# A hybrid decoder layer on one core: norm work moved between two engines, and weight quarters split early and kept in DRAM

## The chip, the cores and the metric

The kernel runs on one core of a Trainium2 chip. The core has five engines that take their instructions in order, each from its own queue, and that meet through semaphores: TensorE (PE in the profile; PEld is its loading of weights), VectorE (DVE), ScalarE (ACT), GpSimd (POOL) and SyncE (SP), which here only issues transfers. ACT and POOL issue transfers too. The metric is the device time of one execution in microseconds, as the median of several runs.

## The reference

The reference computes one layer of a decoder in float32 on 1024 prompt rows and 8 sample rows, which share all weights; the model has 1024 columns. Cut to what matters:

```
x = layer_norm(a * x + 0.5 * swiglu(x, w1_1, w3_1, w2_1))
m = hybrid_mixer(x, states, w_in, ..., w_o)
x = layer_norm(a * x + m)
y = layer_norm(a * x + 0.5 * swiglu(x, w1_2, w3_2, w2_2))

swiglu(x)     = (silu(x @ w1) * (x @ w3)) @ w2          (1024 -> 2816 -> 1024)
layer_norm(x) = (x - mean) * rsqrt(var + eps) * g + b   (over the 1024 columns)
hybrid_mixer: proj = x @ w_in + b_in; an RG-LRU branch (convolution, gates, a linear
  recurrence) and a gated delta-rule branch with 8 heads (convolution, l2 norms, chunked
  recurrence, RMS norm); merged = sum of both, gated; result merged @ w_o
```

New recurrent and convolution states are outputs too, those of the 8 sample rows with a full state matrix per row and head among them.

## The kernel before, in words

**Layout.** All 1032 rows lie along the free dimension and the model's columns along the 128 partitions, as 8 blocks. The rows are cut into three chunks of 344 columns (four of 258 at the end). Activations are kept as a pair XH, XL, a value rounded for TensorE's fast float32 format and the rest; weights are split in the same way, in quarters of 128 × 512 values. A product is three matmuls: high by high, high by low, low by high.

**A weight quarter's way.** In `wload`, SP loads a raw quarter (tile `wraw`, three buffers, 256 KB), ACT copies it rounded into `wh`, and DVE or POOL subtracts to give `wl` (four buffers each). A buffer is written again when its last reader is done. Where `hold` is given, the halves go to tiles that are free at that time.

**Order.** A framework orders the instructions of each engine when the kernel is built, by the order of the program and by ready times that it estimates. Inside an engine's queue nothing overtakes. Generators mix two pieces of work by hand: each `yield` hands over.

**The stages.** (1) SwiGLU 1: two column blocks of its hidden layer (f = 0, 1) as plain products, then 19 blocks f = 2 to 20 with one level of Strassen's algorithm (`strassen`; 7 products of 4 × 2 × 3 matmuls at 258 columns), whose weight sums DVE makes and whose results POOL stores to DRAM. Then `ffnb1`: the hidden values come back in six groups and are multiplied by w2, and the result is gathered in ACC. (2) In the last group, `last_steps` goes chunk by chunk; each chunk has 8 units (one 128-column block m), and after a unit the class `LN` adds the unit to a running sum. The sums of a chunk are closed during the next chunk: `finish` is a generator whose first step takes the mean (a matmul with a tile of ones adds over the partitions, L176), subtracts it, squares and adds up; its second takes the variance total (L176 again); its third normalizes and makes XH and XL. Which unit of the next chunk each step stands behind is set in `last_steps` (units 0 and `LN_STEP` = 4; 5 in SwiGLU 2). The last chunk of norm 1 is closed in `kqv_first`, between the first projections of the mixer. (3) The mixer: 8 heads of the delta rule, mixed with a stream of projections, then the product by w_o with norm 2, again through `last_steps`; each unit there loads two quarters of w_o. `sample`, the single-step recurrence of the 8 sample rows, is a chain of small matmuls pinned in TensorE's order between the units' steps: `wait(n)` lets n slots pass, of which each contraction step of a unit (three matmuls) gives one in the first chunk and two later. (4) SwiGLU 2, like SwiGLU 1 but with f = 0, 1, 2 plain; f = 0 and 1 are computed on two chunks while the third chunk of norm 2 is closed. Norm 3 closes the last group in four chunks; the last of them uses the variant `tail`, with a shorter way to the end.

**Engines in the norms.** The running sum (seven adds for a chunk) is POOL's but for the last add; the squares' adds alternate between DVE and POOL; of the eight splits into XH and XL, those listed in `ON_POOL` have their subtraction on POOL. In the w_o stage the merge's splits (`msplit`) and the weights' subtractions alternate too. POOL also issues the stores of SwiGLU's hidden values, of norm 2's result X2 (eight per chunk, `L232`), and the loads of X2's quarters. The split is `act(h, x, AF.Copy)` at L88 and `tt(l, x, h.bitcast(F32), OP.subtract, eng)` at L91; these helpers give their lines to most steps of the profile.

## Time and profile before

| | |
|---|---|
| median of 3 runs | 2609.95 us (2608.35 to 2614.61) |
| the profiled execution | 2612.26 us |
| its span in the profile | 2610.5 us |
| mean granted TensorE clock | 0.986 |
| busy: TensorE, DVE, ACT, POOL | 2532.2, 1742.9, 1134.0, 467.4 us |
| moved by DMA | 208.65 MB, 80 GB/s in the mean |

The stages in the profiled execution: Strassen blocks of SwiGLU 1 from about 60 to 440 us, the w2 groups to 665, norm 1 with the last w2 group and the first projections from 665 to 746, heads and projections to about 1740, w_o with norm 2 to about 1895, the blocks of SwiGLU 2 to about 2310, w2 and the tail to the end. A busy engine is one with an instruction in it; a matmul at a lower granted clock counts as busy for longer. A step of one tile (128 × 344, for example) is followed by its engine, its source line and the tiles that it reads and writes.

### The profile page before, as it was taken

Reading aid. Unit: us, or ns where it says so; the run is one execution under the profiler, and the core shown is the slowest. Engines: PE = TensorE matmul, PEld = TensorE weight load, DVE = VectorE, ACT = ScalarE, POOL = GpSimd, SP = SyncE. Lnnn points to the kernel's source line nnn. Section 1 sums busy time; section 2 is a strip of 40 time slices with the busy share of each in tenths; the row PEclk is TensorE's granted clock in tenths of the full one; section 3 lists DMA queues with packets and bytes.
Section 4 is the critical chain, followed back from the end, with each engine's and each line's share of the span. In section 5 each row is a group of like instructions: output and inputs, shape, how many; then the busy total and the mean of one; then the engine's idle time right before and its main releaser. Section 6 shows DMA issues by size and latency. Waiting matters only on the chain.

```text
span 2610.5 us, 47260 instructions
## 1 busy us (share of the span) xinstructions
PE 2532.2 (97%) x18374; PEld 2485.7 (95%) x18374; DVE 1742.9 (67%) x3641; ACT 1134.0 (43%) x2426; POOL 467.4 (18%) x633
## 2 busy tenths in 40 slices
PE   9999999999999999999999999998799999999996
PEld 8999999999888999999999999988799999999996
DVE  7666665644696676777767686777766666656446
ACT  5323333221463736565564637635533333332125
POOL 2000000300432112111112121134521111121013
PEclk9999999999998999999999999999899999999998
DMA  6222222432101111111111111124453444333221
GB/s 228 82 76 83 79 79 75 116 98 86 46 30 47 36 49 45 38 50 36 54 37 53 34 57 37 47 89 132 124 154 102 120 123 111 102 117 111 82 69 66
DMA packets 151135, 208.65 MB, mean 80 GB/s; under 512 B 35632, under 2 KB 76080, under 8 KB 150912
## 3 DMA queue, kind: packets, MB, share of 16 engines
q1 hardware_dynamic: 126176, 156.24, 19.6%
q0 software_dynamic: 13904, 43.34, 6.0%
q10 hardware_dynamic: 10832, 6.07, 0.8%
q8 instruction: 144, 2.36, 0.4%
q14 instruction: 79, 0.65, 0.1%
HBM read 164.60 MB, written 40.99 MB: 79 GB/s over the span
## 4 chain that ended last, share of the span: by engine, by line
PE 83%; ACT 6%; DVE 6%; DMA 1%; issue 1%; POOL 1%; ACTq 0%; SPq 0%; DVEq 0%; POOLq 0%
PE ps_mm L132 34%; PE ps_g L132 13%; PE ps_g L298 10%; PE ps_mm L298 10%; PE ps_sq L298 8%; PE ps_g L892 2%; ACT L88 2%; DVE ACC L94 2%; PE ps_sq L778 2%; ACT lnq L88 1%; PE ps_g L778 1%; PE ps_g L784 1%; DVE ACC L91 1%; POOL s L91 1%; DVE wl L91 1%
## 5 line engine op out<-in xcount | busy, mean ns | idle before, releaser
L132 PE MATMUL ps_mm<-XH,wh 128*128 128x344 f32 x1656 | 558.3, 337 | 6.1 <-ACT wh L88 5.8
L132 PE MATMUL ps_mm<-XH,wl 128*128 128x344 f32 x1656 | 532.9, 322 | 0.0
L132 PE MATMUL ps_mm<-XL,wh 128*128 128x344 f32 x1656 | 532.6, 322 | 0.1
L88 ACT ACTIVATE wh<-wraw 128x512 fp32r<-128x512 f32 (+2 forms) x360 | 213.9, 598 | 408.8 <-PE ps_mm L132 140.9
L132 PEld LDWEIGHTS ps_mm<-XH,wh 128*128 128x128 f32 x1656 | 314.4, 190 | 9.6 <-ACT wh L88 5.8
L132 PEld LDWEIGHTS ps_mm<-XL,wh 128*128 128x128 f32 x1656 | 314.4, 190 | 1.8 <-DVE XL L91 0.6
L132 PEld LDWEIGHTS ps_mm<-XH,wl 128*128 128x128 f32 x1656 | 313.8, 190 | 0.4 <-DVE wl L91 0.2
L91 DVE TENSOR_TENSOR wl<-wraw,wh 128x512 fp32r<-128x512 f32 (+3 forms) x339 | 232.3, 688 | 42.5 <-ACT wh L88 38.4
L298 PE MATMUL ps_g<-CH,wh 128*128 128x258 f32 x740 | 209.0, 282 | 0.0
L298 PE MATMUL ps_g<-CH,wl 128*128 128x258 f32 x740 | 208.9, 282 | 0.0
L298 PE MATMUL ps_g<-CL,wh 128*128 128x258 f32 x740 | 208.7, 282 | 0.0
L88 ACT ACTIVATE wh<-S 128x512 fp32r<-128x512 f32 x148 | 93.4, 631 | 197.9 <-PE ps_sq L298 126.8
L298 PE MATMUL ps_mm<-XH,wh 128*128 128x258 f32 x592 | 167.2, 282 | 0.0
L298 PE MATMUL ps_mm<-XH,wl 128*128 128x258 f32 x592 | 166.9, 282 | 0.0
L298 PE MATMUL ps_mm<-XL,wh 128*128 128x258 f32 x592 | 166.8, 282 | 0.0
L353 POOL DMA_DIRECT2D gs<-G x74 | 40.5, 547 | 652.1 <-DVE G L91 604.2
L91 DVE TENSOR_TENSOR wl<-S,wh 128x512 fp32r<-128x512 f32 x148 | 102.3, 691 | 70.9 <-ACT wh L88 70.6
L88 ACT ACT_TABLE_LOAD x109 | 139.8, 1283 | 5.4 <-issue 2.6
L132 PE MATMUL ps_g<-gl,wh 128*128 128x344 f32 x444 | 142.2, 320 | 0.0
L132 PE MATMUL ps_mm<-gl,wh 128*128 128x344 f32 x444 | 142.0, 320 | 0.0
L132 PE MATMUL ps_g<-gh,wh 128*128 128x344 f32 x444 | 142.0, 320 | 0.0
L132 PE MATMUL ps_mm<-gh,wh 128*128 128x344 f32 x444 | 142.0, 320 | 0.0
(536 smaller groups left out, 6884.9 us busy)
## 6 DMA issues: line engine op xcount, KB each, us to landing
wraw<-w SPq DMA_DIRECT2D x164, 256.0 KB, 2.8
wraw<-w_in SPq DMA_DIRECT2D x128, 256.0 KB, 2.6
gr<-gs SPq DMA_DIRECT2D x84, 258.0 KB, 2.8
wr<-w SPq DMA_DIRECT2D x76, 256.0 KB, 2.6
gs<-G POOLq DMA_DIRECT2D x74, 258.0 KB, 2.6
wraw<-w_o SPq DMA_DIRECT2D x40, 256.0 KB, 2.8
x<-ACC POOLq DMA_DIRECT2D x24, 172.0 KB, 2.2
y<-ACC SPq DMA_DIRECT2D x32, 129.0 KB, 1.9
```

The lines of the kernel that those rows point to most:

```text
L88: return S.activation(out, in_, f, **kw)
L91: return (eng or V).tensor_tensor(out, a, b, op=op)
L94: return V.scalar_tensor_tensor(out, a, s, b, op0=op0, op1=op1)
L132: PE.matmul(p, a, b, start=(n == 0), stop=(n == 3 * nk - 1))
L298: PE.matmul(ps_[c], a[:, k, :], b, start=(start and n == 0), stop=(n == 11), skip_group_check=not start)
L353: G.dma_start(gs[f][:, s], x)
L778: x = PE.matmul(ck(p, i), a, b, start=True, stop=True)
L784: x = PE.transpose(ck(p, i), a, IDT)
L892: pin(PE.matmul(o[r, c, :], a(c), b(c), start=True, stop=True))
```

## The change

- `LN.add` and `finish`: every running sum and every add of squares is DVE's. `ON_POOL` is gone: all subtractions that make XL are DVE's. In norm 1 all eight blocks take the shorter form that four of them had (ACT makes XH with the bias, one fused DVE step makes XL). The deviation `rs` takes a buffer of the ring `s1` (three) instead of `mu`'s only one, except in the tail.
- `last_steps`: the mean step stands behind unit 1 (before: 0), the variance and normalizing steps behind unit 6 in all norms (before: 4, and 5 in SwiGLU 2). In SwiGLU 2's plain blocks the steps of the open norm stand in the first chunk of f = 0 and of f = 1. The first projections are reordered so that three products, not two, precede the variance total.
- `presplit`: after each of the 19 Strassen blocks of SwiGLU 1, two weight quarters are loaded by SP, split by ACT and DVE in the usual rings, and both halves are stored by POOL to DRAM (256 KB each). The 38 quarters are: 8 of w2_1's last group, 6 of w_in (the first head's k, q and v), 16 of w_o, 8 of w1_2 and w3_2 for f = 0 and 1.
- `fetch`: where these quarters are used, POOL loads both halves straight into `wh` and `wl` or into the held tiles: 124 transfers of 256 KB, 80 of them in w_o, where quarters are loaded again in each chunk. The raw loads, rounding copies and subtractions at these places are gone.
- The subtractions of w2_2's last group and of the merge are all DVE's. The five waits of the sample chain grow (12 to 16, 6 to 14, 6 to 14, 8 to 16, 6 to 14 slots).

```diff
-LN_STEP = 4
+LN_STEP = 6
-ON_POOL = (1, 3, 5, 7)
...
+    def whl(n=4):
+        return [wp.tile([128, n, 128], F32R, name=x, tag=x, bufs=4) for x in ("wh", "wl")]
+
+    def presplit(quads):
+        for key, src in quads:
+            raw = wp.tile([128, 4, 128], F32, name="wraw", tag="wraw", bufs=3)
+            nc.sync.dma_start(raw, src)
+            h, l = whl()
+            split(h, l, raw)
+            halves[key] = dr.tile([2, 128, 4, 128], F32R, name="hv", tag="hv" + key)
+            for i, x in enumerate((h, l)):
+                G.dma_start(halves[key][i], x)
+            yield
+
+    def fetch(key, nq=2, hold=None):
+        hl = []
+        for q in range(nq):
+            h, l = hold(4) if hold else whl()
+            for i, x in enumerate((h, l)):
+                G.dma_start(x, halves[key + "_%d" % q][i])
+            hl += [(h[:, k, :], l[:, k, :]) for k in range(4)]
+        return hl
...
+        ws = [quads("w2%d" % m, A["w2_1"][m][:, g[0]:g[0] + 4], 1) for m in range(KD)]
+        ws += [quads("in%d" % b, A["w_in"][b]) for b in (KC, QC, VC)]
+        ws += [quads("o%d" % m, A["w_o"][m]) for m in range(KD)]
+        ws += [quads("w%d%d" % (i, f), A["w%d_2" % i][f]) for f in range(2) for i in (1, 3)]
...
-                tt(self.s1, self.ys[0], y, OP.add, G)
-            elif 2 < n < (KD - 1 if self.tail else KD):
-                tt(self.s1, self.s1, y, OP.add, G)
-            elif n == KD and not self.tail:
-                tt(self.s1, self.s1, y, OP.add, V)
+                tt(self.s1, self.ys[0], y, OP.add)
+            elif 2 < n < (KD - 1 if self.tail else KD + 1):
+                tt(self.s1, self.s1, y, OP.add)
...
-                    tt(q[k % 2], q[k % 2], q[k], OP.add, (V, G)[k % 2])
+                    tt(q[k % 2], q[k % 2], q[k], OP.add)
...
-            rs = third("mu", w)
+            rs = third("mu" if self.tail else "s1", w)
...
-                if i in ON_POOL or self.gi == 2:
+                if self.gi == 2:
                     act(y, y, AF.Identity, bias=b_)
-                    split(h, l, y, G if i in ON_POOL else V)
-                    if self.gi == 2:
-                        G.dma_start(X2[:, k, self.s], y)
+                    split(h, l, y)
+                    G.dma_start(X2[:, k, self.s], y)
                     continue
...
+            if n == 2 and f < 2:
+                return [fetch("w%d%d" % (i, f), hold=hold) for i in (1, 3)]
...
-                if fin and f == 0 and t < 2:
-                    for _ in range(1 + t):
+                if fin and t == 0 and f < 2:
+                    for _ in range(1 + f):
                         next(fin)
...
                     strassen(f, w1, w3, up, cx, store)
...
+                    for _ in range(2 if pre else 0):
+                        next(pre, None)
...
-                            held[m] = w2load(m, eng=(V, G)[m % 2], hold=hold if n == 2 or m < 6 else None)
+                            if n == 1:
+                                held[m] = fetch("w2%d" % m, 1, hold if m < 6 else None)
+                            else:
+                                held[m] = w2load(m, hold=hold)
...
-                if fin and i == 0:
+                if fin and i == 1:
                     next(fin)
-                if fin and i == LN_STEP + (out is not None):
+                if fin and i == LN_STEP:
...
-                wk, wq = (wload(A["w_in"][b0], KD) for b0 in (KC, QC))
-                wv = wload(A["w_in"][VC], KD, hold=hold)
+                wk, wq = (fetch("in%d" % b0) for b0 in (KC, QC))
+                wv = fetch("in%d" % VC, hold=hold)
...
                 kq(0, 1)
+                kq(0, 2)
                 kq(1, 0)
                 next(fin)
                 next(fin)
                 kq(1, 1)
-                kq(0, 2)
...
-                    split(h[:, :n], l[:, :n], ACC[:, k, t * TC:t * TC + n], (V, G)[k % 2])
+                    split(h[:, :n], l[:, :n], ACC[:, k, t * TC:t * TC + n])
...
-                    recent[m] = wload(A["w_o"][m], KD, eng=(V, G)[m % 2])
+                    recent[m] = fetch("o%d" % m)
...
-        yield from wait(12)
+        yield from wait(16)
...
-        yield from wait(6)
+        yield from wait(14)
```

More of the change, by code (lines that the diff above doesn't have):

```diff
@@ L124, in wload, with quads, early_list @@
         return hl
+    halves = {}
+    def whl(n=4):
[18 more added lines that the diff above has]
+        return hl
+    def quads(key, src, n=2):
+        return [(key + "_%d" % q, src[:, 4 * q:4 * q + 4]) for q in range(n)]
+    def early_list():
+        g = GROUPS[-1]
+        ws = [quads("w2%d" % m, A["w2_1"][m][:, g[0]:g[0] + 4], 1) for m in range(KD)]
+        ws += [quads("in%d" % b, A["w_in"][b]) for b in (KC, QC, VC)]
+        ws += [quads("o%d" % m, A["w_o"][m]) for m in range(KD)]
+        ws += [quads("w%d%d" % (i, f), A["w%d_2" % i][f]) for f in range(2) for i in (1, 3)]
+        return [q for w in ws for q in w]
     def mm3_steps(p, w, xs, nk):
@@ L386, in ffn @@
             make = combos(up, *((A["x"], 2) if n == 1 else (X2, 0)))
+            pre = presplit(early_list()) if n == 1 else None
             spare = ["S"] * 3 + ["wr"] * 3 + ["s0", "rb"]
@@ L1246, in sample @@
         V.tensor_copy(KE[:, 0], K_)
-        yield from wait(6)
+        yield from wait(14)
         pq = psum("sq")
@@ L1274, in sample @@
         tt(M, OS, OS, OP.mult)
-        yield from wait(8)
+        yield from wait(16)
         pn = psum("sq")
@@ L1286, in sample @@
         nc.scalar.dma_start(RTD, rt)
-        yield from wait(6)
+        yield from wait(14)
         pn = psum("sq")
```

## The prediction, made before the changed kernel was run

> **What bounds the kernel now.** I read the page's first part, then a table of stretches, then the list of what the engines waited for, and last the groups and the timeline inside the stretches that are not full. From the page:
>
> ```profile
> span 2610.5 us, 47260 instructions
> PE 2532.2 (97%) x18374; PEld 2485.7 (95%) x18374; DVE 1742.9 (67%) x3641; ACT 1134.0 (43%) x2426; POOL 467.4 (18%) x633
> ```
>
> TensorE sets the time. It idles 2610.5 − 2532.2 = 78 us, and no edit here takes a matmul away, so the gain lies inside those 78 us and in the clock granted around them. The stretches that the change touches (columns: us, then busy PE, PEld, DVE, ACT, POOL with counts, granted clock, DMA share, GB/s):
>
> ```profile
> 60.00:440.00 380.00, 380.00 (x3165) 380.00 (x3164) 238.62 (x444) 121.26 (x231) 20.20 (x38) 1.00 0.24 77
> 665.00:746.00 81.00, 69.63 (x401) 65.68 (x401) 66.73 (x112) 46.55 (x85) 43.27 (x43) 0.97 0.16 47
> 1740.00:1895.00 155.00, 128.18 (x752) 121.63 (x751) 109.94 (x185) 80.07 (x173) 81.97 (x88) 0.90 0.39 121
> 2565.00:2610.50 45.50, 25.96 (x155) 23.14 (x153) 27.50 (x65) 26.64 (x56) 14.29 (x20) 0.82 0.21 70
> ```
>
> The first row is the Strassen blocks of SwiGLU 1: TensorE full at full clock, so they have nothing to give and can only lose. Norm 1 (665 to 746) idles 81 − 69.63 = 11.4 us and loses about 0.03 × 69.63 = 2.1 us to the clock: 13.5 us at stake. Norm 2 with the w_o stage (1740 to 1895) idles 26.8 us and loses 0.10 × 128.18 = 12.8 us: 39.6 us. The tail idles 19.5 us, much of it the closing chain of the last chunk. What TensorE waited for, over the span (line, releaser, us in total, times, longest), then L176 alone in norm 1 and in the tail:
>
> ```profile
> PE ps_sq L176 <- DVE s L91: 28.7, 12, 7.6
> PE ps_g L132 <- DVE wl L91: 4.8, 3, 4.1
> PE ps_sq L1238 <- DVE St L1233: 4.3, 1, 4.3
> PE ps_sq L1277 <- DVE kt L91: 1.9, 1, 1.9
> PE ps_mm L132 <- DVE m_lt L91: 1.6, 1, 1.6
> ...
> PE ps_sq L176 <- DVE s L91: 7.6, 4, 2.5
> ...
> PE ps_sq L176 <- DVE s L91: 10.2, 5, 4.8
> ```
>
> Two thirds of this is L176, the partition totals of the norms, which wait for sums; the rest is the sample group's small matmuls and weight splits. The largest single wait, 7.6 us, is the last variance total of norm 2. From the timeline (start, us, engine, step, and in brackets the idle time before it), what stood ahead of it:
>
> ```profile
> 1872.04 0.69 DVE L91 TENSOR_TENSOR w1S<-wraw,w1wr 128x512 fp32r<-128x512 f32 x1 [5.44 <-ACT w1wr L88]
> ...
> 1875.05 5.45 POOL L91 TENSOR_TENSOR s<-s,lnq 128x344 f32<-128x344 f32 x3 [10.59 <-ACT lnq L88]
> ```
>
> DVE stood 5.44 us behind the split of one of SwiGLU 2's first weights, whose raw load was late, and then POOL needed 5.45 us for three adds. Both causes are things that the change removes.
>
> **The change, part by part.** First, additions and splits move from POOL to DVE. Groups in norm 1 (the first six rows), in norm 2 (four) and over the span (the last):
>
> ```profile
> L91 POOL TENSOR_TENSOR s<-s,ACC 128x344 f32<-128x344 f32 x15 | 14.8, 986 | 2.6 <-DVE ACC L94 1.8
> L91 POOL TENSOR_TENSOR s<-s,lnq 128x344 f32<-128x344 f32 x9 | 10.7, 1184 | 17.1 <-ACT lnq L88 16.9
> L94 DVE SCALAR_TENSOR_TENSOR ACC<-ACC,LNT,mu 128x344 f32<-128x344 f32 x16 | 12.1, 793 | 0.6 <-ACT mu L88 0.6
> L91 DVE TENSOR_TENSOR ACC<-ACC,mu 128x344 f32<-128x344 f32 x24 | 14.0, 629 | 0.8 <-ACT mu L88 0.8
> L91 DVE TENSOR_TENSOR wl<-wraw,wh 128x512 fp32r<-128x512 f32 x5 | 4.6, 929 | 3.6 <-ACT wh L88 3.6
> L91 DVE TENSOR_TENSOR w2h<-wraw,w2h 128x512 fp32r<-128x512 f32 x3 | 3.4, 1174 | 0.8 <-ACT w2h L88 0.8
> ...
> L94 DVE SCALAR_TENSOR_TENSOR ACC<-ACC,LNT,mu 128x344 f32<-128x344 f32 x24 | 20.1, 886 | 3.8 <-ACT mu L88 3.8
> L91 DVE TENSOR_TENSOR wl<-wraw,wh 128x512 fp32r<-128x512 f32 x18 | 17.5, 974 | 5.6 <-ACT wh L88 5.6
> L91 POOL TENSOR_TENSOR wl<-wraw,wh 128x512 fp32r<-128x512 f32 x15 | 20.4, 1363 | 6.6 <-ACT wh L88 4.7 <-ACT r L88 1.9
> L91 DVE TENSOR_TENSOR s<-s,s 128x344 f32<-128x344 f32 x3 | 1.5, 509 | 0.8 <-POOL s L91 0.8
> ...
> L88 ACT ACTIVATE wh<-wraw 128x512 fp32r<-128x512 f32 (+2 forms) x360 | 213.9, 598 | 408.8 <-PE ps_mm L132 140.9
> ```
>
> A 128x344 add costs POOL 986 to 1184 ns and DVE 509 ns undisturbed. Beside POOL's work DVE's own steps are long: 793 and 886 ns for a fused multiply that has the same shape as the 509 ns add.
>
> So DVE pays for the moved work and gets some back. Norm 1, from the rows: a chunk moves 6 sums, 3 square adds and 4 splits, 39 steps in three chunks × 0.51 = +19.9 us. Back come the stretched parts, 16 × (0.793 − 0.51) + 24 × (0.629 − 0.51) = 7.4 us, and the weight splits, now fetched: 4.6 + 3.4 = 8 us. DVE's 66.73 us becomes about 71, in a stretch that I expect to fall from 81 to about 71. DVE is then full, fuller than now, and only because some of its steps (the first projections' evacuations and convolutions) can run later does that not cost the whole gain: what is gained comes from order. A mean total after unit 1 and a variance total after unit 6, instead of units 0 and 4, leave 1 and 2 units more (12 matmuls of 0.16 us, 1.9 us each: the blocks' 380 us over 3165 matmuls are 0.12 us at 258 columns, so 0.16 at 344) for sums that today are up to 2.5 us late. A rest stays: the fetch that opens the last w2 group waits for ring slots as the split did (I leave 2 us for it), and about 1.5 us of late sums. 13.5 − 3.5 = **−10 us** (bounds −5, half, and −13.5, all).
>
> Norm 2: of DVE's 109.94 us, 17.5 go with the splits of w_o, and 24 × (0.886 − 0.51) = 9 us of stretch; 25 sums, 11 splits and 7 merge splits come, 43 × 0.51 = 22 us. DVE ends near 105, no higher than now. The 7.6 us wait loses both causes, since the two weight pairs behind it are fetched. The waits on weight splits (4.8) go. The sample chain's 4.3 and 1.9 us go, since each of its steps gets 14 to 16 slots for 6 to 12: what was late had 4.3 us to make good, and 8 slots of two per contraction step are 4 × 0.47 = 1.9 us in chunks two and three and 3.8 us in the first, so perhaps 1 us is left. The 8-column splits (1.6 and two smaller, 2.6 together) stay. Against it stand the fetches, below, at 4 us, with 2 us of the clock that no idle time explains: 39.6 − 1 − 2.6 − 4 − 2 = **−30 us** (bounds −12 and −38).
>
> Second, the fetches. Each unit of w_o takes four POOL-issued transfers of 256 KB, none of which the trace has; the nearest rows:
>
> ```profile
> gs<-G POOLq DMA_DIRECT2D x74, 258.0 KB, 2.6
> s<-S POOLq DMA_DIRECT2D x16, 256.0 KB, 5.4
> u<-x POOLq DMA_DIRECT2D x6, 258.0 KB, 4.6
> rb<-rtd POOLq DMA_DIRECT2D x16, 256.0 KB, 7.6
> ...
> L353 POOL DMA_DIRECT2D gs<-G x74 | 40.5, 547 | 652.1 <-DVE G L91 604.2
> ```
>
> An issue costs POOL 0.55 us: four per unit are 2.2 of the 3.8 us that 24 matmuls take (24 × 0.16); the eight X2 stores per chunk add 4.4 us in 30. POOL is free for that, since it loses its sums and splits (20.4 us for the weights alone). A slot of the ring of four frees 1.5 units, 5.7 us, before its next contents are read; two issues take 1.1, so a landing under 4.6 us is hidden. The bounds of a landing are 2.6 and 7.6 us; I take 3.5, between the store of the same size (2.6) and the reads of four chunked rows (4.6), since a weight quarter lies in one piece per partition. 1 MB in 3.8 us is 278 GB/s, over twice the stretch's mean of 121, so now and then one will be late: the 4 us above.
>
> The Trainium skill (DMA: Bandwidth & Descriptors, "SWDGE vs HWDGE vs iDMA") says that a transfer into a float32r tile always counts as a cast, which only GpSimd's software path does. It prices no cast, and no transfer of this trace is one. Its fit for a software transfer, 2.0 us plus bytes/436e3, would make 2.6 us of 256 KB, an estimate by which the 4 us would be near zero and the time 2565.
>
> Third, the presplit in SwiGLU 1. Each of 19 blocks gets two loads on SP's queue, two ACT copies (0.6 us), two DVE subtracts (0.69) and four POOL stores (2.2 us of issue). A block lasts 380/19 = 20.0 us; DVE goes from 12.6 to 14 us of it, ACT from 6.4 to 7.6, POOL from 1.1 to 3.3, DMA from 77 to about 155 GB/s.
>
> ```profile
> ACT wh L88 <- PE ps_sq L298: 85.0, 38, 2.3
> ACT wh L88 <- PE ps_g L298: 44.2, 20, 2.3
> ACT wh L88 <- PE ps_mm L298: 35.6, 36, 1.3
> ```
>
> These waits of 60 to 440 us show ACT waiting 165 us for TensorE to free ring slots: splits run as far ahead as the four slots allow, about three products of 2.9 us. A presplit pair holds its slot for 0.6 + 0.69 + 1.1 + 2.6 = 5 us and frees it without TensorE, two per block. The lead shrinks to about one product and is not used up: **+2 us** (bounds 0 and +10, half a microsecond per block). If the cover were gone, each block would pay the overhang.
>
> Fourth, the tail: the last group's subtracts and the sums move to DVE, and the deviation no longer shares the single buffer of the mean. The 10.2 us in five waits shrink, but not the 4.8 us of the last chunk, whose variant keeps its POOL steps: **−3 us** (0 to −6). The reordering of the first projections, and the regrouped steps in SwiGLU 2's plain blocks, cost nothing: TensorE takes the same matmuls in another order.
>
> Sum: −10 − 30 + 2 − 3 = −41. The profiled execution took 2612.26 us (1.76 around its span), 2.3 above the median of 2609.95: 2571.3 for it, **2569** for the median. Measurement tells 0.3%, 7.8 us, from no change.
>
> **The rivals.** *DVE is the new bound.* All elementwise work of the norms queues on one engine, 71 us of work against a stretch that should shrink to 71. For it: the evacuations of PSUM stand in the same queue, so that late sums hold TensorE's buffers too. Against: norm 2 is only two thirds full. Half of both norm gains is lost: 2569 + 20 = 2589.
>
> *Fetches land late* (the slower side). Place: 20 loads in w_o and the eight of w2. With a landing of L us each waits L − 4.6 us. At 5.4 (row s<-S) that is 28 × 0.8 = 22 us, less the 4 counted: 2587; at 7.6 (row rb<-rtd) 28 × 3 − 4 = 80 us: 2649. The kernel turns slower than the bound of 2617.8 when the price passes 49 us, at L of about 6.5. For it: POOL takes its queue in order, so a fetch that waits for a slot also holds the X2 stores and the sample group's power step. Against: no write or read of this size and of long rows comes near 6.5.
>
> *POOL's issues are held up by DVE.* If they stretch as the three adds at 1875 us did (5.45/3 = 1.8 us each), four need 7.2 us of a unit's 3.8: 20 × 3.4 = 68 us, 2637. The Trainium skill (SBUF — State Buffer, "Who interferes with whom") has a rule by which this would come: GpSimd writes the descriptors through the port that VectorE's two-port steps hold, so a busier DVE starves POOL's transfers. The trace does not show it so far: 547 ns per issue of gs<-G, most of them in blocks in which DVE is 63% busy (238.62 of 380).
>
> *The ring stalls Strassen 1.* If two extra pairs cost more than the lead, a block loses about a split's latency, 1 to 2 us: 19 to 38 us, 2588 to 2607. Against it stand the 165 us of waiting for slots, which are slack.
>
> *It doesn't do what it says:* the totals still wait, because what they wait for is the last add behind ACT's squares, not POOL. Then only the weight and sample waits go: 4.8 + 4.3 + 1.9 + 7.6 = 18.6 us and about a third as much of clock (12.8 over 26.8 idle, less what stays), some 25 us: 2585.
>
> **How the numbers follow.** Forecast (2552 to 2580): 0.50. DVE bound: 0.15. Totals still late: 0.10. Strassen stalls: 0.08. Fetches late: 0.12, of it 0.07 up to 2602, 0.02 within 7.8 us of before and 0.03 past it. Issues held up: 0.05, 0.02 of it within the bound (a milder stretch) and 0.03 past it. Faster: 0.50 + 0.15 + 0.10 + 0.08 + 0.07, less 0.03 for the upper end of the Strassen case, 0.87; same 0.03 + 0.02 + 0.02 = 0.07; slower 0.06. The range runs from 2550, where norm 1 gives all and norm 2 most of its stake, to 2602, which takes in the first three cases, most of the fourth and the mild late fetches.
>
> **What would show it.** Right: waits of L176 on DVE sums under 10 us in all; no wait on wl or St in w_o; clock of the norm 2 stretch at 0.95 or more; the stretch 60 to 440 still full; POOL adds gone, and DVE's fused multiply at 0.51 us. Wrong: fetch landings over 4.6 us with TensorE waiting on wh in w_o; idle time inside the blocks of SwiGLU 1; DVE over 95% busy through norm 1 with L176 still waiting.

## The result, and the profile after

The changed kernel takes 2578.5 us (median of 4 runs, 2569.2 to 2583.1) against 2610.6 us for the kernel before in the same comparison: a ratio of 0.9871 with a 95% interval from 0.9839 to 0.9903, 32 us faster. The forecast was 2569, the range 2550 to 2602. The profiled execution took 2575.4 us; its span is 36.9 us shorter than before.

From the page of the changed kernel:

```profile
span 2573.6 us, 47385 instructions
PE 2520.0 (98%) x18374; PEld 2474.6 (96%) x18374; DVE 1729.5 (67%) x3767; ACT 1115.5 (43%) x2390; POOL 418.5 (16%) x683
```

TensorE has the same 18374 matmuls and now idles 53.6 us instead of 78. The stretches, with the columns as before (us, busy PE, PEld, DVE, ACT, POOL, granted clock, DMA share, GB/s); the first two are the same stretches as before, the third is the second part of norm 1, and the last two are cut anew, since w_o and the tail now come earlier:

```profile
60.00:440.00 380.00, 379.94 (x3162) 379.73 (x3162) 254.81 (x482) 145.09 (x269) 60.83 (x113) 1.00 0.51 155
665.00:746.00 81.00, 76.88 (x466) 72.34 (x465) 64.96 (x143) 37.95 (x68) 12.68 (x26) 1.00 0.27 79
700.00:746.00 46.00, 44.50 (x272) 41.77 (x271) 43.77 (x98) 31.53 (x56) 5.36 (x12) 1.00 0.20 58
1710.00:1900.00 190.00, 182.24 (x1161) 177.69 (x1162) 116.98 (x274) 75.85 (x174) 78.36 (x144) 0.98 0.75 215
2551.00:2573.60 22.60, 7.09 (x17) 3.91 (x16) 13.41 (x34) 15.64 (x34) 2.90 (x4) 0.64 0.28 94
```

The Strassen blocks are as full as before with three times POOL's work and twice the traffic in them. Norm 1 idles 4.1 us of 81 instead of 11.4, at full clock. Norm 2 and w_o idle 7.8 us of 190 at a clock of 0.98. What TensorE still waits for (line, releaser, us in total, times, longest; L209 is the former L176):

```profile
PE ps_sq L209 <- DVE s L90: 6.9, 6, 2.3
...
PE ps_mm L167 <- DVE m_pre L90: 3.3, 1, 3.3
...
PE ps_mm L330 <- DVE wl L90: 2.7, 1, 2.7
PE ps_g L167 <- DMA w2h<-hv: 2.4, 2, 2.2
...
PE ps_sq L1302 <- DMA hM<-S: 1.7, 2, 1.4
PE ps_sq L1302 <- DMA hP<-S: 1.7, 2, 1.1
```

The waits for the norms' sums fell from 28.7 to 6.9 us, 5.5 of them in the tail. New are small waits for transfers: the first fetched weight of the last w2 group (2.2 us) and the sample group's states (3.4 us together). The DVE groups of norm 2 and the fetches:

```profile
L93 DVE SCALAR_TENSOR_TENSOR ACC<-ACC,LNT,s 128x344 f32<-128x344 f32 x24 | 12.4, 571 | 8.6 <-ACT s L87 8.6
...
L90 DVE TENSOR_TENSOR s<-s,ACC 128x344 f32<-128x344 f32 x18 | 9.2, 512 | 0.3
```

```profile
L146 POOL DMA_DIRECT2D wl<-hv x50 | 27.1, 541 | 5.0 <-PE ps_mm L167 3.2 <-DMA w2h<-hv 0.9 <-PE ps_g L167 0.5
```

```profile
wh<-hv POOLq DMA_DIRECT2D x50, 256.0 KB, 3.8
wl<-hv POOLq DMA_DIRECT2D x50, 256.0 KB, 3.9
hv<-wh POOLq DMA_DIRECT2D x38, 256.0 KB, 2.6
hv<-wl POOLq DMA_DIRECT2D x38, 256.0 KB, 3.7
...
w2h<-hv POOLq DMA_DIRECT2D x12, 256.0 KB, 5.9
```

DVE's fused multiply takes 571 ns where it took 886 in norm 2 beside POOL's splits. A fetch lands 3.8 us after its issue (the burst of twelve at the last w2 group: 5.9), and the issue costs 0.54 us.

Where the 36.9 us of the span went, between matmuls that both traces have (the first of the last w2 group, of head 0, of w_o, of SwiGLU 2's Strassen blocks, of its last w2 group):

| us | before | after | difference | forecast |
|---|---|---|---|---|
| start to last w2 group | 665.28 | 667.91 | +2.6 | +2 (and 2 left at that start) |
| norm 1 with the first projections | 120.99 | 110.91 | −10.1 | −10, that start included |
| heads | 929.91 | 931.18 | +1.3 | 0 |
| w_o, norm 2, SwiGLU 2's plain blocks | 227.84 | 203.22 | −24.6 | −30 |
| SwiGLU 2 to its last w2 group | 587.60 | 588.24 | +0.6 | 0 |
| last group and tail | 78.86 | 72.16 | −6.7 | −3 |

### The profile page after: what moved, and what is told of

Read it like the earlier page. It is cut to its first block, busy times and chain, and to the rows that moved or that the text cites. A ratio compares the mean times of both kernels' runs of the same rounds, so it can differ in the third digit from the quotient of the medians.

```text
span 2573.6 us, 47385 instructions
## 1 busy us (share of the span) xinstructions
PE 2520.0 (98%) x18374; PEld 2474.6 (96%) x18374; DVE 1729.5 (67%) x3767; ACT 1115.5 (43%) x2390; POOL 418.5 (16%) x683
## 3 DMA queue, kind: packets, MB, share of 16 engines
q1 hardware_dynamic: 122720, 149.95, 19.1%
## 5 line engine op out<-in xcount | busy, mean ns | idle before, releaser
L87 ACT ACTIVATE wh<-wraw 128x512 fp32r<-128x512 f32 (+2 forms) x348 | 206.8, 598 | 392.9 <-PE ps_mm L167 139.4
L90 DVE TENSOR_TENSOR wl<-wraw,wh 128x512 fp32r<-128x512 f32 (+2 forms) x348 | 232.8, 672 | 64.9 <-ACT wh L87 28.6
L167 PE MATMUL ps_mm<-gh,wl 128*128 128x344 f32 x444 | 141.9, 320 | 0.0
L167 PE MATMUL ps_g<-gh,wl 128*128 128x344 f32 x444 | 141.8, 319 | 0.0
```

What stands on the lines that cost most here:

```text
L87: return S.activation(out, in_, f, **kw)
L90: return (eng or V).tensor_tensor(out, a, b, op=op)
L167: PE.matmul(p, a, b, start=(n == 0), stop=(n == 3 * nk - 1))
```

## The experiments

All twelve compute the whole result. Each kernel was measured together with the kernel before, and a ratio is between these two; the medians of the kernel before were 2611.8, 2610.4 and 2611.0 us in the three groups of runs. The changed kernel was measured in a group of its own, so a difference from its 2578.5 us is one between groups. The stage times are from one profiled execution of each kernel, between the matmuls of the table above. How far such a time can be trusted shows in the six profiles whose kernels have the changed kernel's steps in norm 1 and in the tail: norm 1 takes 110.6 to 111.3 us in them and the tail 71.3 to 72.4. In w_o and norm 2 the same code gives 203.2 to 210.3 us, at different granted clocks.

### The norm part alone, and the weight part alone

The first kernel leaves the weights as before:

```diff
-            pre = presplit(early_list()) if n == 1 else None
+            pre = None
...
-                    recent[m] = fetch("o%d" % m)
+                    recent[m] = wload(A["w_o"][m], KD, eng=(V, G)[m % 2])
```

> Only the norm part of the change: sums, square adds, XL splits and merge splits on DVE, later totals, the deviation in the ring s1, the new order of the first projections; no presplit and no fetch, weights of w_o and of the last w2 group split as before, old waits of the sample chain. Theory A (the parts add up, as the prediction's sum has it): the norms' L176 waits and the stretched DVE steps go, the waits on weight splits and the sample chain's stay: about 16 us faster than before, 2594 (2588 to 2600). Theory B (the moved work needs the room that the weight splits leave on DVE): DVE runs full in both norms, 69 + 8 us of work in norm 1's 81, the totals wait as long as before: 2606 to 2622, no gain or a loss.

The second leaves the norms as before:

```diff
-LN_STEP = 6
+LN_STEP = 4
...
-                tt(self.s1, self.s1, y, OP.add)
+                tt(self.s1, self.s1, y, OP.add, G)
```

> Only the weight part: 38 quarters split in the Strassen blocks and fetched later; sums and splits on POOL as before, totals behind units 0 and 4 as before, old waits of the sample chain. Theory A: the waits on weight splits and the late raw load of SwiGLU 2's first weights go with their clock, L176 still waits in norm 1 and in the tail: some 20 us faster, 2590 (2584 to 2597). Theory B: the same gain or more, since POOL and DVE are both relieved by the splits: 2580 to 2590, and then the norm part is worth under 10 us on top of it.

Measured: the norm part 2589.1 us, 22.7 faster than before (ratio 0.9913, 0.9898 to 0.9928); the weight part 2596.8, 15.0 faster (0.9945, 0.9926 to 0.9964). The product of the ratios is 0.9858, the whole change 0.9871: the parts add up (theory A), and the norm part is the larger one. The moved work does not need the room of the weight splits as theory B had it. But the stages show where each part needs the other. TensorE's waits with the norm part alone:

```profile
PE ps_g L167 <- DVE wl L90: 6.5, 2, 5.3
...
PE ps_mm L167 <- DVE ACC L93: 5.3, 1, 5.3
PE ps_sq L1273 <- DVE St L1268: 3.6, 1, 3.6
...
PE ps_sq L1312 <- DVE kt L90: 2.7, 1, 2.7
```

and with the weight part alone:

```profile
PE ps_sq L212 <- DVE s L91: 20.3, 10, 4.8
...
PE ps_mm L168 <- DMA wl<-hv: 3.6, 2, 3.4
```

With the norms alone, norm 1 gains 4.2 us (116.75), and the waits on splits and on the sample chain stay. The wait of 5.3 us in it is for an evacuation on DVE. In the trace the steps that DVE takes right ahead of that evacuation are the norm's own, and in the 30 us before it DVE makes no weight split; why the wait is gone with the fetches is open. With the weights alone norm 1 gains nothing (122.51) and the tail nothing (80.33). In w_o and norm 2 they give 8.6 and 19.1 us, more together (27.7) than the whole change in its profile (24.6); that difference is within what this stage varies by.

### Places or engine

One kernel keeps all work on DVE and puts the norm's steps back to their old places; the other keeps the places and puts the sums back on POOL:

```diff
-                if fin and i == 1:
+                if fin and i == 0:
...
-                if fin and i == LN_STEP:
+                if fin and i == LN_STEP + (out is not None):
```

> The changed kernel with the norm's steps at their old places: mean total behind unit 0, variance total behind unit 4 (5 in SwiGLU 2), the old order of the first projections, the old places in SwiGLU 2's plain blocks; all sums stay on DVE. Theory order (the prediction: what norm 1 gains comes from order): L176 waits come back in norm 1, w_o and the tail, some 15 us or more with their clock, 2592 to 2602. Theory engine (a DVE that does not share with POOL is fast enough for the old places): under 5 us slower than the changed kernel, 2578 to 2584.

```diff
-                tt(self.s1, self.s1, y, OP.add)
+                tt(self.s1, self.s1, y, OP.add, G)
...
-                    tt(q[k % 2], q[k % 2], q[k], OP.add)
+                    tt(q[k % 2], q[k % 2], q[k], OP.add, (V, G)[k % 2])
```

> The changed kernel with the running sums and every second add of squares back on POOL; splits stay on DVE and the totals at their later places. Theory order: the later places give POOL's slower adds the time that they need, little comes back: 2579 to 2586. Theory engine: POOL's adds block DVE's steps (0.51 us to 0.8) and reach the totals late, also because POOL's queue now holds the fetches: 2590 to 2605, with the fused multiply of the norm stretches above 0.6 us again.

Measured together: old places 2576.0 us, ratio 0.9869 (0.9853 to 0.9885), the same as the changed kernel; sums on POOL 2593.9, ratio 0.9929 (0.9914 to 0.9943). The engine is what counts, not the place. The kernel with the weight part alone, which has the norms' splits on POOL too and the old places, took 2596.8 us; its interval overlaps that of the sums on POOL, so no further price of the splits or of the places can be told. Waits with the old places, then with the sums on POOL:

```profile
PE ps_sq L209 <- DVE s L90: 4.6, 3, 3.0
```

```profile
PE ps_sq L211 <- DVE s L90: 13.0, 8, 3.3
```

Of these 13.0 us, 4.0 are in norm 1 (1.4 in the changed kernel) and 9.0 in the tail (5.5). In w_o and norm 2 no total waits. What TensorE waits for there are fetches, which stand in the same queue as the adds:

```profile
PE ps_g L167 <- DMA wl<-hv: 3.1, 4, 1.5
PE ps_mm L167 <- DMA wl<-hv: 1.8, 2, 1.6
```

With those for `wh` (1.3) they are 6.2 us, against 0.8 in the changed kernel and 4.6 in the worst of the kernels without these adds that have the same fetches. Three groups of norm 1 (665 to 740 us) with the sums on POOL, then the first of them in the changed kernel:

```profile
L90 DVE TENSOR_TENSOR ACC<-ACC,mu 128x344 f32<-128x344 f32 x23 | 14.5, 678 | 0.7 <-ACT mu L87 0.7
...
L93 DVE SCALAR_TENSOR_TENSOR ACC<-ACC,LNT,s 128x344 f32<-128x344 f32 x16 | 8.6, 586 | 0.0
...
L90 POOL TENSOR_TENSOR s<-s,lnq 128x344 f32<-128x344 f32 x7 | 8.1, 1161 | 19.1 <-issue 10.1 <-ACT lnq L87 8.9
```

```profile
L90 DVE TENSOR_TENSOR ACC<-ACC,mu 128x344 f32<-128x344 f32 x24 | 10.8, 508 | 0.2 <-ACT mu L87 0.2
```

My expectation named two signs for the engine theory. The totals come late, since an add takes POOL 1161 ns. The fused multiply did not become long, it stays at 586 ns; another step of DVE did, the subtraction of the mean, with 678 ns in place of 508. So the sums on POOL cost in both ways, and the sign that I named was on the wrong step. The trace shows why: a fused multiply is long only where a POOL add or subtraction is under way beside it. In the kernel before, the 31 of shape 128 × 344 without one took 567 ns in the mean, the ten beside a POOL subtraction that makes XL 1247 ns, and the five beside an add of a running sum 760 ns. With only the sums on POOL, three of 48 fall beside an add (565, 842 and 1340 ns). The kernel with the weight part alone, which has sums, XL splits and merge splits on POOL but fetches its weights, has them long again, over the span:

```profile
L94 DVE SCALAR_TENSOR_TENSOR ACC<-ACC,LNT,mu 128x344 f32<-128x344 f32 x48 | 34.1, 758 | 14.2 <-ACT mu L88 14.2
```

### The sample chain's waits

```diff
-        yield from wait(16)
+        yield from wait(12)
...
-        yield from wait(14)
+        yield from wait(6)
```

> The changed kernel with the sample chain's five waits as before (12, 6, 6, 8, 6 slots in place of 16, 14, 14, 16, 14). Theory chain (the prediction: the chain's stalls went because each step got more slots): its 4.3 and 1.9 us waits on St and kt come back with their clock, 2584 to 2592. Theory engines (they went because POOL's power step and DVE's small steps no longer stand behind POOL adds and weight splits): within 3 us of the changed kernel, 2574 to 2582, with waits on St and kt of under 1.5 us each.

Measured: 2575.1 us (2563.0 to 2578.9), ratio 0.9848 (0.9816 to 0.9880): no loss. What was a wait of 4.3 us for St is

```profile
PE ps_sq L1278 <- DVE St L1273: 0.7, 1, 0.7
```

and the wait for kt at the later step is gone. The chain was not held up by too few slots. The two halves of the change, which both have the old waits, show what did it: with the norm part alone the waits stay (3.6 and 2.7 us, shown above), and with the weight part alone, whose adds are still POOL's, no wait of the chain on St or kt is above 0.2 us. So of theory engines the weight splits in w_o were the cause, and POOL's adds were not.

### Twice as much in the Strassen blocks

```diff
-                    for _ in range(2 if pre else 0):
+                    for _ in range(4 if pre else 0):
```

(the list holds each quarter twice).

> The changed kernel with four quarters presplit per Strassen block instead of two (each of the 38 is split and stored twice, to its own place; the copy is never read). The prediction's rival in the blocks of SwiGLU 1 was that extra pairs use up the lead of the ring of four. Theory cover (slack far from used up; ACT 38% and DVE 67% busy in the blocks of the changed kernel): the 19 blocks stay full, within 5 us of the changed kernel, 2573 to 2585. Theory edge (two pairs already use nearly all of the lead): each block loses 1 to 3 us, 20 to 57 us, 2595 to 2640, with TensorE waiting for wh or wl inside the blocks.

Measured: 2602.5 us (ratio 0.9961, 0.9942 to 0.9979). The stretch of the blocks, and the wait in them, over the span:

```profile
60.00:440.00 380.00, 368.71 (x3009) 363.75 (x3009) 261.56 (x496) 152.50 (x291) 95.78 (x179) 1.00 0.71 221
```

```profile
PE ps_mm L330 <- DVE wl L90: 10.9, 15, 3.0
```

Of the 10.9 us, 7.9 in 14 waits are in the blocks; the longest, 3.0, is at the first Strassen block of SwiGLU 2. The last matmul on a weight combination (`ps_g<-CH,wl` of block 20) starts at 454.8 us instead of 434.5, 1.1 us later for each of 19 blocks, while no engine but TensorE is near full and the DMA share is 0.71. The time is that of theory edge, but its reason, that two pairs already use up the lead, is not shown: two cost nothing that the trace shows (434.45 us before and after), four cost 1.1 us per block. Nor does the trace show a lead that is used up at four. ACT's waits for TensorE to free ring slots (60 to 440 us), which the prediction took as the slack, are 165 us before, 119 with two quarters and still 110 with four. What stops the blocks at four is open.

### The fetches: issues, queue and cast

Twice the issues for the same bytes, in w_o only:

```diff
+                if key[0] == "o":
+                    for j in (0, 2):
+                        G.dma_start(x[:, j:j + 2], halves[key + "_%d" % q][i][:, j:j + 2])
+                    continue
```

> The changed kernel with each of w_o's 80 transfers cut into two of 128 KB, so that POOL issues eight per unit: the same bytes, twice the issues. The prediction's rival of late fetches priced this as issue time over unit time: 8 x 0.55 = 4.4 us against a unit's 3.8, 0.6 us for each of 20 units. Theory issue-bound: 10 to 18 us slower than the changed kernel, 2588 to 2597, with TensorE waiting for transfers in w_o. Theory slack (the smaller transfers land sooner, and chunks two and three start with two units that load nothing): under 5 us, 2576 to 2584.

Measured: 2587.7 us in two runs (2582.1 and 2593.2), w_o with norm 2 at 222.96 us instead of 203.22. POOL's issues, and TensorE's waits for the transfers:

```profile
L148 POOL DMA_DIRECT2D wl<-hv x80 | 44.3, 577 | 3.7 <-issue 2.8 <-PE ps_g L171 0.8
```

```profile
PE ps_mm L171 <- DMA wl<-hv: 5.6, 6, 2.7
...
PE ps_g L171 <- DMA wl<-hv: 1.8, 4, 0.7
```

Eight issues of 0.577 us are 4.6 us of a unit's 3.8: 0.8 us for 20 units, 16 us, of which 9 (medians, whose intervals overlap) to 20 (this stage of the profiles) are seen. TensorE's waits for these transfers rose from 0.8 to 8.1 us, and the rest of the stage's 20 is within its spread. The runs agree with the rule of the rival, issue time over unit time; the changed kernel with its four issues (2.2 us) lies on the safe side of it.

The next two change only how the 80 transfers of w_o are issued: from SP, as plain float32 copies, and from POOL, as plain float32 copies.

```diff
-                G.dma_start(x, halves[key + "_%d" % q][i])
+                nc.sync.dma_start(x.bitcast(F32), halves[key + "_%d" % q][i].bitcast(F32))
```

> The changed kernel with the 80 transfers of w_o issued from SP's queue, as plain float32 copies of the same bytes, instead of from POOL's as float32r. Theory queue (in w_o a POOL in whose queue fetches wait for ring slots, 60 us of waiting in the profile, holds up the stores of X2 and the sample group's power step): 3 to 10 us faster in w_o, 2568 to 2576. Theory neutral (TensorE waits for fetches only 0.8 us in w_o of the changed kernel): within 3 us, 2575 to 2582. SP's queue also holds the loads of S0 and of SwiGLU 2, so it may also come out some 5 us slower.

> The changed kernel with the 80 transfers of w_o as plain float32 copies, still issued from POOL. It separates the cast from the queue: if the float32r form is what makes a fetch land at 3.8 us, against 2.6 for a plain store from POOL and 2.9 for a raw load from SP, the landing in w_o falls to about 2.7; if it stays near 3.8, the cast costs nothing and the landing is a matter of load. The time stays within 4 us of the changed kernel by both.

Measured: from SP 2572.5 us, ratio 0.9845 (0.9824 to 0.9866); plain from POOL 2578.5 (two runs). The landings in w_o and norm 2 (1700 to 1900 us), from SP and then plain from POOL:

```profile
wh<-hv SPq DMA_DIRECT2D x38, 256.0 KB, 3.7
wl<-hv SPq DMA_DIRECT2D x38, 256.0 KB, 3.9
```

```profile
wh<-hv POOLq DMA_DIRECT2D x42, 256.0 KB, 3.8
wl<-hv POOLq DMA_DIRECT2D x42, 256.0 KB, 3.9
```

Neither the float32r form nor POOL's queue makes a fetch slower: all three forms land at 3.7 to 4.0 us in this stretch. The medians put the version from SP 6 us ahead of the changed kernel, but the intervals overlap. From SP, w_o itself ended 5.5 us sooner, which is no more than it differs by between profiles of the same code (126.0 to 133.0 us from its first to its last matmul), and the blocks after it took 4.8 us more (82.0 us, against 77.2 to 78.4 in those profiles); TensorE then waited for raw weights at the start of SwiGLU 2 (waits of 1840 to 1920 us):

```profile
PE ps_mm L334 <- DVE wl L90: 3.4, 1, 3.4
PE ps_mm L334 <- ACT wh L87: 2.2, 1, 2.2
```

### Toward a faster version

Two waits of the list above have a remedy in the order of the work:

```diff
-held[m] = fetch("w2%d" % m, 1, hold if m < 6 else None)
+held[m] = fetch("w2%d" % m, 1, hold if m > 1 else None)
...
-[up_, up_, [6, 7] + up_[:6]]
+[up_, up_, up_]
...
-                if t == NT - 2 and i == KD - 1:
+                if t == NT - 2 and i == KD - 2:
                     for _ in side[0]:
```

> The changed kernel with two more edits: in SwiGLU 1's last group the first two weights go to the ring of four and the other six to held tiles (before: the last two), with all chunks in the order 0 to 7, so that the first fetch needs no tile of the group before; and in w_o the last eight columns are split behind unit 6 of the second chunk, ahead of the normalizing steps on DVE, and not behind unit 7. Theory: the 2.2 us wait at the group's start and the 3.3 us wait at the start of w_o's third chunk go, with some clock: 5 to 8 us faster than the changed kernel, 2570 to 2574. Rival: the waits come back one step later (the fetches of units 2 and 3; the sample chain's end, drained by force): within 2 us.

Then SwiGLU 2's norm steps at their old places, and in the last kernel the low halves of w_o from SP as well:

```diff
-                if fin and i == 1:
+                if fin and i == (out is None):
...
-                if fin and i == LN_STEP:
+                if fin and i == LN_STEP - (out is not None):
```

> The two further edits of the run before (ring tiles for the first two weights of SwiGLU 1's last group; the last eight columns split behind unit 6) and, in SwiGLU 2 alone, the norm's steps at their old places, behind units 0 and 5. From the run with all old places, whose end came 2.2 us sooner after the start of that group: 2 us less than the run without it, 2563 to 2570. Rival: no difference that can be told, 2566 to 2574.

```diff
-                G.dma_start(x, halves[key + "_%d" % q][i])
+                y = halves[key + "_%d" % q][i]
+                if key[0] == "o" and i:
+                    nc.sync.dma_start(x.bitcast(F32), y.bitcast(F32))
+                else:
+                    G.dma_start(x, y)
```

> The same, with w_o's low halves issued from SP as plain float32 copies and the high halves from POOL. With all of them on SP w_o ended 5.5 us sooner and SwiGLU 2's first blocks 4.8 us later, since their raw loads stood behind on SP. Theory: half on each queue keeps part of the first and little of the second, 2 to 4 us less than the run without it, 2560 to 2568. Rival: the two cancel again, within 2 us of it.

Measured: 2568.7 us (0.9838, 0.9812 to 0.9864), 2571.4 (0.9850, 0.9827 to 0.9874) and 2565.1 (0.9824, 0.9803 to 0.9845). In all three, head 0 starts 3.1 to 4.2 us sooner than in the changed kernel (774.6 to 775.7 us instead of 778.8): the last w2 group starts 2.0 to 2.9 us sooner, and norm 1 takes 109.6 to 109.8 us instead of 110.9. That edit works, and the 2.2 us wait is gone. The wait on m_pre left the list, but w_o did not become shorter by it alone (205.8 and 211.8 us). The old places in SwiGLU 2 are worth about 1 us in the tail (71.71 and 70.94), which the medians can't tell. With two queues w_o and norm 2 took 197.4 us, the shortest of all, at full clock up to 1820 us:

```profile
1701.00:1820.00 119.00, 116.17 (x761) 111.49 (x761) 73.27 (x188) 36.16 (x98) 30.21 (x56) 1.00 0.76 223
```

TensorE's idle time in that stage is 7.0 us, against 8.6 and 9.5 in the two versions before it, so the second queue shows about 2 us there; the rest goes with the granted clock (0.99 against 0.96 and 0.94), and which of it is the edit's is not shown.

This version, 2565 us, beats the kernel before by 46 us. Against the changed kernel it is 13 us by the medians of different groups; their intervals just overlap (0.9845 and 0.9839), so that part is likely and not settled.

## Why the prediction was right or wrong

**Right** were the bound (TensorE's idle time and clock in two norms and the tail), the sign, the size within a third, and the sum to 4 us in the profile: −41 forecast, −36.9 in the trace. The median moved by 32. The signs named for the forecast came: L176's waits under 10 us (6.9), no wait on St or wl in w_o above 0.5 us, a clock of 0.98 there, full Strassen blocks, and the fused multiply short (571 ns; I had set 510 from an add of the same shape, so 0.06 us of each step that I counted as stretched was its own). That the sum came within 4 us is in part luck: the tail gave 3.7 us more than its term and norm 2 gave 5.4 less, and the stage of norm 2 differs by 7 us between profiles of the same code.

**Norm 1: −10 forecast, −7.5 with the start of the last group.** The size was near, the step was wrong: "what is gained comes from order". With the old places nothing is lost (2576.0 us); with the sums on POOL 15 us are, by the medians of two groups of runs, and in the profiles norm 1 (120.29 against 110.91, 9.4) and the tail (5.2) make up that much. The 9.3 us by which w_o and norm 2 are longer there are not counted: 212.5 us is near the 210.3 that the changed kernel's code takes in another profile. In place of the order: an add on POOL takes twice as long as on DVE, a total waits for a chain of them, and beside them DVE's own steps are longer. The totals are 2.6 of the 5.4 us by which TensorE's idle time in norm 1 grows (from 3.2 to 8.6); the rest are waits for a fetch, for an evacuation and for head 0's first step, and the clock falls to 0.96.

**The full DVE.** The rival had 71 us of work in 71. DVE was busy 43.77 of 46 us from 700 to 746, 95%, and TensorE 44.50: its one wait there was 1.4 us. But DVE was nearly as full there before, with TensorE at 37.12:

```profile
700.00:746.00 46.00, 37.12 (x209) 35.15 (x208) 42.87 (x74) 31.80 (x60) 24.17 (x25) 0.94 0.08 25
```

A full engine cost nothing as long as what was late on it was work that nobody waited for. And the sum of DVE's work had the wrong sign. From the last group's first matmul to head 0, DVE was busy 103.0 of 121.0 us before and 96.0 of 110.9 after; with the norm part alone 105.5. So the moved work cost it 2.5 us there and not 19.9 − 7.4 = 12.5: more steps than the two groups that I counted had been stretched beside POOL (the last add of the squares, `s<-s,s`, fell from 971 to 504 ns). That the steps fit only because the weight splits left was half right: without the fetches norm 1 took 116.75 us, with a 5.3 us wait for an evacuation on DVE, which no weight split shortly ahead of it explains.

**Norm 2: −30 forecast, −24.6.** The waits that were to go went. The whole stage (columns as above) before and after, then in two experiments with the changed kernel's steps in this stage, the doubled presplit and the plain copies from POOL:

```profile
1716.18:1944.02 227.84, 200.69 (x1227) 193.41 (x1226) 161.43 (x276) 107.62 (x231) 108.31 (x124) 0.93 0.43 133
1710.00:1913.22 203.22, 192.72 (x1223) 187.97 (x1224) 129.65 (x297) 81.66 (x185) 79.99 (x147) 0.97 0.72 206
1732.08:1941.55 209.47, 198.59 (x1223) 193.04 (x1224) 129.78 (x297) 81.54 (x185) 80.02 (x148) 0.95 0.70 200
1708.30:1918.62 210.32, 202.02 (x1224) 197.43 (x1225) 129.74 (x296) 81.55 (x185) 80.28 (x147) 0.93 0.63 199
```

TensorE's idle time fell from 27.2 to 10.5 us (10.9 and 8.3 in the other two); of the −30, 19.2 were idle time. The other 8 us are granted clock, of which I had counted 10.8, and they are the part that does not repeat: at as little idle time and a lower clock the stage takes up to 210.3 us, so the same code also shows a gain of 18. That the sample chain's waits went because of longer waits was wrong: with the old ones they stay away, and the weight part alone takes them away. What was not in the sum are two waits: the states of the sample group land late beside the fetches (3.4 us), and the split at SwiGLU 2's first Strassen block (2.7 us), which had no wait before. The eight-column splits, 2.8 us before, cost 3.3.

**The fetches: +4 us forecast.** A landing of 3.8 to 3.9 us against the 3.5 that I took, under the 4.6 that are hidden; waits for fetches of 0.8 us in w_o and 2.4 at the last w2 group. The 4 us were for w_o, where 0.8 came: the term was too large by most of it, unless the sample group's late states (3.4 us) are counted with it. The Trainium skill (DMA: Bandwidth & Descriptors, "SWDGE vs HWDGE vs iDMA") says that such a transfer counts as a cast; no run here shows that it does, but if so it has no price: the plain copies land at the same 3.8 and 3.9 us. The fit that the prediction took from the Trainium skill, an estimate of 2.6 us, holds for the stores of the high halves (2.6, row hv<-wh), and neither for those of the low halves, issued right behind them (3.7, row hv<-wl), nor for the loads under w_o's traffic of 215 GB/s. *POOL's issues held up by DVE* did not occur: 541 ns each beside a DVE that works on all sums. The rule that the prediction took from the Trainium skill for this case speaks of VectorE's two-port steps; whether the moved adds and subtractions are such steps, no run here shows.

**Strassen 1: +2 forecast, nothing measured.** Two quarters per block were covered, and four were not, at 1.1 us a block. That it was the lead of the ring which covered them, and that its size was judged right, is not shown: ACT's waits for ring slots are nearly as long at four as at two.

**The tail: −3 forecast, −6.7.** The term was too small: I gave the gain to fewer late sums but took the last chunk's 4.8 us as fixed. The norm part alone gives all of it (72.09), the weight part none, and the running sums, which leave POOL in the last chunk too, are 5.2 us of it (77.39 with the sums on POOL). The waits in it fell from 10.2 to 5.5 us, the longest from 4.8 to 2.3. Later places hurt here by 1 to 2 us: 69.96 us with all old ones, 70.94 with the old ones in SwiGLU 2 alone, against 71.71 without. That the last steps of chunk three then stand in the closing chain is the likely reason and was not tried.

## What to carry to other kernels

When a total waits for a chain of small adds, the engine's time per add can count before the place of the total: try the engine first, and ask whether a slower helper engine in the chain helps or only makes it longer, and what its work does to the steps beside it. A transfer queue filled by a compute engine was safe here with issues of 2.2 us per unit of 3.8 and was not with 4.6; compute that ratio before looking at bandwidth. Idle slots under a full TensorE are real room for preparing later weights, up to some limit, and doubling the dose shows on which side of it a kernel stands. A gain in one profile is to be split into idle time and granted clock before it is put down to an edit.

## What was not expected of the hardware

**The granted clock differs over the same work.** The runs of the changed kernel spread over 14 us, those of the kernel before over 6 (over 10 in a group of ten runs), and the mean clock goes with the time: 0.988 in the run of 2583.1 us, 0.992 in those of 2575.4 and 2569.2. The same piece of head 0, with the same waits ahead of it (1.3 and 1.4 us on one transfer), in the changed kernel and in the first of the faster versions:

```profile
819.00:849.00 30.00, 28.69 (x227) 26.59 (x225) 11.70 (x24) 8.12 (x16) 5.25 (x5) 0.72 0.08 21
```

```profile
815.00:845.00 30.00, 28.61 (x277) 27.02 (x276) 15.42 (x32) 15.76 (x29) 5.35 (x6) 1.00 0.09 22
```

At the same busy time TensorE did 227 matmuls at a clock of 0.72 and 277 at 1.00; head 0's first thousand matmuls take 153.5 us and 146.2, about 7 us apart. In the sample group's part of w_o it is the other way round, 1755 to 1785 us in the same two kernels:

```profile
1755.00:1785.00 30.00, 26.91 (x192) 25.91 (x193) 12.51 (x27) 7.14 (x22) 7.71 (x16) 1.00 0.89 244
```

```profile
1755.00:1785.00 30.00, 28.59 (x161) 28.08 (x160) 10.76 (x28) 3.50 (x14) 6.89 (x13) 0.77 0.70 194
```

More idle time, full clock; less, 0.77. In ten-microsecond slices both dips reach 0.50 and are over within some 30 us, and neither has a wait longer than 1.5 us in the 30 us ahead of it. The heads, which no edit here touches, vary from 923.6 to 932.6 us over all profiles. So the heads and the stage of w_o are known to about 7 us only from one profiled execution, and an edit worth less there has to be read from its waits, or from several runs; norm 1 and the tail repeat within about 1 us. What decides whether a dip comes was not tried. The Trainium skill (TensorE: Matmul & The Clock Gate, "Part 1: The HAM clock gate") has the clock set by the activity in a free-running window of about 3.4 us, which would let a shift of a few hundred nanoseconds decide; neither dip here followed an idle stretch of this length, and no run here tests the rule.
